# Attention kernel: the row shift as one fp16 row, the closing norm on VectorE in halves, output weights loaded two ahead

## The chip, the cores and the metric

The kernel runs on one core of one Trainium2 chip. The metric is the device time of one execution in microseconds. The kernel before takes 1215.45 us, the median of three runs (1214.27 to 1218.1). One other execution was recorded by the hardware profiler; all views of the profile are of that one.

The engines of the core are called as in the profile: PE (TensorE: matmuls; PEld its weight loads), DVE (VectorE), ACT (ScalarE), POOL (GpSimd) and SP (SyncE, which here only issues DMAs). SP's instructions run in the order of its one queue: an instruction that waits holds up those behind it.

## The reference

One layer of a mixer with two branches: an adaptive layer norm, one input projection, a gated linear recurrence (RG-LRU) on one half of the channels and an attention with a forget gate on the other half, an output projection, a gated residual and a closing layer norm. S = 2048 tokens, D = 1024, eight heads of 64. What the change touches is the attention, the gate on the output weights and the closing norm:

```python
    def block(bi):                      # 128 queries of one block, all heads
        ...
        s = jnp.einsum('bhqd,bhkd->bhqk', qb, k).astype(jnp.float32) * scale
        s = s + (dq[..., :, None] - d_cum[:, :, None, :])
        ...
        s = jnp.where(mask, s, NEG_INF)
        p = jax.nn.softmax(s, axis=-1)
        return jnp.einsum('bhqk,bhkd->bhqd', p.astype(v.dtype), v)
...
        y = jnp.concatenate([y_r, y_a], axis=-1) @ w_out[l]
        res = DEEPNORM_ALPHA * x.astype(jnp.float32) + gate[:, None, :].astype(jnp.float32) * y.astype(jnp.float32)
        x = (_layer_norm(res) * ln_gain[l].astype(jnp.float32) + ln_bias[l].astype(jnp.float32)).astype(dtype)
```

## The kernel before

**Stages.** Up to some 540 us the kernel normalizes x, projects it, runs the recurrence, and writes keys, values, queries and gates to scratch in DRAM (`kd`, `kb`, `vd`, `qd`, `zd`, `yd`). From some 540 us on it runs the attention. Queries are taken in four chunks `ci` of 512 tokens; within a chunk the eight heads `h` come one after the other, 32 items (ci, h) in all. A chunk `ci` sees (ci + 1) x 512 keys.

**One item.** `maxpass` loads the keys of the head: `kk[:, 0]` from `kd` (128 rows of fp16, line 1241) and `kk[0:68, 1]` from `kb` (68 rows, line 1242), then the queries `qb` (line 1243) and `qs` (line 1245). All of these go through SP's queue. The 68 rows of `kb` are 64 rows of the key's head plus four that belong to the row shift and to the forget gate: two rows of the constant RS (written once from `crow`) and two rows `ndr` of the decay, high and low part. The matmuls `pmx` score queries against keys from fp16 parts, VectorE takes each row's maximum (`mc`, line 1259), and lines 1267 to 1269 make the shift of each row: `trow` in fp32, its fp16 high part as column 64 of `Z`, and the rest as column 65. Four transposing matmuls `pzt` bring both columns into rows, and ScalarE copies them into rows 64 and 65 of `qb` (line 1277). These two rows times the RS rows of `kk` then subtract the maximum within the score matmul of `s_t` (`pst<-qb,kk`, 66 rows deep). ScalarE takes the exponential (`pf`, line 1290) and its fp16 part (`ph`, line 1292), GpSimd the low part for three of four tiles (line 1294), VectorE for the fourth (line 1296), and `acc` multiplies by the values.

**Buffers.** Scores, maxima and transposes share five PSUM banks of the tag A. `kk` comes from the pool `r4` (eight buffers of 4 KB per partition) while `ci` is below 2, later from a pool of larger tiles. `r4` also holds the weight tiles `woraw`, the gate `gbc`, the residual tiles `xres` and the gain and bias of the closing norm (`lng`, `lnb`), so that a new tile there waits until the tile that held the buffer is done with.

**Output weights.** `wout_gen` (line 976 on) is a side chain that runs among the first items of the attention. `wo_raw` loads 128 rows of `w_out` (512 KB) and multiplies them by the gate on GpSimd (line 1003); ScalarE and VectorE then split the product into two fp16 parts (lines 880, 881). The next tile is loaded and multiplied before the present one is split: one ahead. `gate_gen` makes the gate itself earlier (adds of line 957).

**Output projection and closing norm.** From some 730 us on, `out_gen` weaves the output projection into the attention, a tile of 128 tokens at a time: `zs` loaded from `zd` (line 1346), multiplied with the transposed attention output on VectorE (line 1369), matmuls `pout`, the residual (line 1468), then `ln_gen`: statistics on VectorE, the reciprocal root on GpSimd (line 1395), `nm` on VectorE (line 1384), the normalization on ScalarE (line 1385, 1024 columns), gain and bias on GpSimd (lines 1387, 1388, 1024 columns each), and the store (line 1389). Fifteen tiles go this way; the last one goes through `out_last`, which does its gain and bias on VectorE.

**What sets the order.** The instructions of each engine stand in the order in which a scheduler places them at build time; the generators above give it the work in the order of their yields, and `issue_after` pins some of it behind a named instruction. VectorE, like every engine, then works in that order: an operation that waits holds up all behind it on its engine.

Of the kernel before, what the change touches and what calls it, by code (L numbers as in the profile page):

```python
# [14 lines left out]
ALU = mybir.AluOpType  # L15
# [23 lines left out]
def hybrid_mixer(  # L39
# [63 lines left out]
            tick()  # L103

    kd = dr.tile([H, P, S], F16, name="kd", tag="kd")
    kb = dr.tile([H, 68, S], F16, name="kb", tag="kb")
    vd = dr.tile([S, C], F32, name="vd", tag="vd")
    qd = dr.tile([H, P, S], F16, name="qd", tag="qd")
    zd = dr.tile([4, P, S], F32, name="zd", tag="zd")
# [755 lines left out]
    nc.vector.tensor_scalar(L8p, sp, 8.0, None, ALU.mult)  # L865
    crow = r4([2, S], "crow", F16)
    nc.vector.memset(crow, RS)
    nc.scalar.dma_start(kb[:, DH:DH + 2, :].rearrange("h a s -> a h s"), crow.unsqueeze(1).broadcast_to([2, H, S]))
    QB = [cst([68, CH], f"qb{i}", F16) for i in range(4)]
    Z = [cst([P, 4, 68], f"Z{i}", F16) for i in range(4)]  # L870
    for q in QB:
        nc.scalar.dma_start(q[66:68, :], crow[:, 0:CH])
    for z in Z:
        nc.gpsimd.memset(z, 0.0)

# [66 lines left out]
    def gate_gen():  # L942
        for k in range(KT):
            raw = r4([P, D], "woraw")
            nc.sync.dma_start(raw, w_out_v[k])
            nc.vector.tensor_reduce(out=wocol[:, k:k + 1], in_=raw, axis=AX.X, op=ALU.max, apply_absolute_value=True)
            if k % 2 == 1:
                yield
        acc = None
        for k in range(KT):  # L950
            w = r4([P, D], "wgate")
            nc.sync.dma_start(w, w_ada_v[k, :, 2 * D:3 * D])
            nc.scalar.activation(w, w, AF.Copy, scale=cact[:, k:k + 1])
            if acc is None:
                acc = w
            else:
                nc.gpsimd.tensor_tensor(out=acc, in0=acc, in1=w, op=ALU.add)
            if k % 2 == 1:
                yield
        gbc = r4([P, D], "gbc")  # L960
        nc.sync.dma_start(gbc, b_ada[0, 2 * D:3 * D].partition_broadcast(P))
        for n in range(2):
            sl = slice(n * CH, (n + 1) * CH)
            ps = bank("C", "pgt")
            mm(ps, ones, acc[:, sl], True, True)
            nc.vector.tensor_tensor(gbc[:, sl], ps, gbc[:, sl], ALU.add)
        gate["bc"] = gbc
        yield
        cols = sm([P, 2], "amg")
        col_max(g_col, AX.X, cols[:, 0:1])  # L970
        col_max(gbc, AX.X, cols[:, 1:2])
        chains.append(gate_fin(cols))
        yield
# [10 lines left out]
    def wout_gen():  # L984
        gbc = gate["bc"]
        wm = sm([P, KT], "wm")
        nc.vector.tensor_tensor(wm, wocol, mk, ALU.mult)
        col = col_max(wm)
        yield
        yield  # L990
        am = yield from all_max(col)
        am_w = sm([P, 1], "am_w")
        nc.vector.tensor_scalar(am_w, am, TINY, gate["am"], ALU.max, ALU.mult)
        scales(am_w, RS, sc_o[:, 1:2], sc_o[:, 0:1])
        nc.vector.tensor_scalar(kap, sc_o[:, 1:2], 1.0 / YT, None, ALU.mult)
        so = cst([P, KT], "so")
        nc.vector.tensor_tensor(so, g_col, mk, ALU.mult)
        nc.vector.tensor_scalar(so, so, sc_o[:, 0:1], 1.0 / ALPHA, ALU.mult, ALU.mult)
        yield
        def wo_raw(k):  # L1000
            raw = r4([P, D], "woraw")
            nc.sync.dma_start(raw, w_out_v[k])
            nc.gpsimd.tensor_tensor(out=raw, in0=raw, in1=gbc, op=ALU.mult)
            return raw

        nxt = wo_raw(0)
        yield
        for k in range(KT):
            raw = nxt
            if k + 1 < KT:  # L1010
                nxt = wo_raw(k + 1)
            w = wh([P, 2, D], "wo") if k < KT - 1 else r4([P, 2, D], "wo", F16)
            for n in range(2):
                sl = slice(n * CH, (n + 1) * CH)
                split_out(w[:, 0, sl], w[:, 1, sl], raw[:, sl], so[:, k:k + 1])
                yield
            wo.append(w)

# [66 lines left out]
    def decay_gen():  # L1085
# [37 lines left out]
        nc.vector.tensor_tensor(ndr[:, 1], ndf, ndr[:, 0], ALU.subtract)  # L1123
        for h in range(H):
            for a in range(2):
                nc.sync.dma_start(kb[h, DH + 2 + a, :].rearrange("(t p) -> t p", p=P), ndr[h * TT:(h + 1) * TT, a, :])
        yield

    dg = decay_gen()
# [101 lines left out]
    def maxpass(ci, h, res):  # L1231
# [10 lines left out]
        nc.sync.dma_start(kk[0:68, 1, 0:nk], kb[h, :, 0:nk])
        nc.sync.dma_start(qb[0:DH, :], qd[h, DH:P, sl])
        qs = sb.tile([P, CH], F16, name="qs", tag="qs", bufs=3)
        nc.sync.dma_start(qs, qd[h, :, sl])
        nc.gpsimd.memset(qb[DH:DH + 2, :], 0.0)
        res.append((kk, qb, qs))
        yield
        mc = sm([P, 4, 4], "mc")
        for i in range(4):  # L1250
            nk = (4 * ci + i + 1) * P
            for b in range(ci + 1):
                w = min(CH, nk - b * CH)
                ps = bank("A", "pmx")
                end = b == ci
                mm(ps[:, 0:w], qb[:, i * P:(i + 1) * P], kk[0:68, 1, b * CH:b * CH + w], True, not end)
                if end:
                    mm(ps[:, w - P:w], identb, maskn, False, True)
                nc.vector.tensor_reduce(out=mc[:, i, b:b + 1], in_=ps[:, 0:w], axis=AX.X, op=ALU.max)  # L1259
                yield  # L1260
# [2 lines left out]
            nc.vector.tensor_reduce(out=m, in_=mc[:, :, 0:ci + 1], axis=AX.X, op=ALU.max)  # L1263
        else:
            m = mc[:, :, 0]
        t = sm([P, 4], "trow")
        nc.vector.tensor_scalar(t, m, -1.0 / RS, ndc[:, ci, h:h + 1], ALU.mult, ALU.add)  # L1267
        nc.vector.tensor_copy(z[:, :, DH], t)  # L1268
        nc.vector.tensor_tensor(z[:, :, DH + 1], t, z[:, :, DH], ALU.subtract)  # L1269
        yield True  # L1270
        yield True
        with tc.issue_after(last["pe"]):
            ps = bank("A", "pzt")
            for i in range(4):
                mm(ps[0:DH + 2, i * P:(i + 1) * P], z[:, i, 0:DH + 2], ident16, i == 0, i == 3, True)
        yield
        nc.scalar.copy(qb[DH:DH + 2, :], ps[DH:DH + 2, :])

    def s_t(ci, h, kt, kk, qb, qs):
        q0 = max(0, kt - 4 * ci) * P  # L1280
# [2 lines left out]
        ps = bank("A", "pst")  # L1283
        mm(ps[:, 0:w], kk[:, 0, ks], qs[:, q0:CH], True, False)
        md = kt >= 4 * ci
        mm(ps[:, 0:w], kk[0:DH + 2, 1, ks], qb[0:DH + 2, q0:CH], False, not md)
        if md:
            mm(ps[:, 0:P], maskn, identb, False, True)
        pf32 = t2([P, CH], "pf32")
# [84 lines left out]
    def ln_gen(tt, xt):  # L1374
        st = sm([P, 2, 6], "bst")
        nc.vector.bn_stats(st[:, 0, :], xt[:, 0:CH])
        yield
        nc.vector.bn_stats(st[:, 1, :], xt[:, CH:D])
        mv = sm([P, 2], "mv")
        nc.vector.bn_aggr(mv, st)  # L1380
        rs = ln_rs(mv)
        yield
        nm = sm([P, 1], "nm")
        nc.vector.scalar_tensor_tensor(nm, mv[:, 0:1], -1.0, rs, ALU.mult, ALU.mult)
        nc.scalar.activation(xt, xt, AF.Identity, scale=rs, bias=nm)  # L1385
        yield
        nc.gpsimd.tensor_tensor(out=xt, in0=xt, in1=late["lng"], op=ALU.mult)
        nc.gpsimd.tensor_tensor(out=xt, in0=xt, in1=late["lnb"], op=ALU.add)
# [230 lines left out]
```

## Time and profile before

| | |
|---|---|
| median of three runs | 1215.45 us (1214.27 to 1218.1) |
| the profiled execution | 1211.64 us |
| its span in the profile | 1209.9 us |
| mean clock granted to TensorE | 0.966 |
| HBM traffic | 97.66 MB read, 31.59 MB written |

A line of the profile that groups instructions reads: line, engine, operation, `out<-in` by the program's names, shape, count | busy us, mean ns of one | idle us of the engine just before them, and what ended most of it. In a list of waits a row reads: engine and line `<-` what it waited for: us in total, times, longest. A row of the timeline reads: start us, us, engine, line, operation, and in square brackets the idle time before it and its releaser. A row of a table by stretches reads: from:to, its length, then busy us of PE, PEld, DVE, ACT and POOL (with instruction counts), the clock granted to TensorE, the mean busy share of the 16 DMA engines, and GB/s. Idle time of an engine that is not the bound costs nothing by itself.

### The profile page before, as it was taken

What the parts mean: (1) busy time and instruction counts of PE and PEld (TensorE: products, weight loads), DVE (VectorE), ACT (ScalarE), POOL (GpSimd) and SP (SyncE); (2) the same over time, 40 slices, a digit from 0 to 9 for tenths busy, and PEclk for the clock granted to TensorE, in tenths of its full rate; (3) what the DMA queues carried; (4) which work ended last, traced back from release to release, by engine and by line L of the source; (5) the groups of instructions that cost most, each with busy time, mean ns of one, the idle gap of its engine ahead of it and who ended that gap; (6) DMA issues with size and microseconds to landing.
All of it is one profiled execution on the core that took longest, in us unless ns stands there. A gap on an engine that the chain in (4) does not pass through costs nothing. (4 is left out here: it accounts for less than half of the span.)

```text
span 1209.9 us, 20217 instructions
## 1 busy us (share of the span) xinstructions
PE 1111.2 (92%) x7467; PEld 622.8 (51%) x7467; DVE 767.7 (63%) x1435; ACT 719.6 (59%) x1244; POOL 686.0 (57%) x670
## 2 busy tenths in 40 slices
PE   6997899999999899999979979989999989999787
PEld 6874444454444444434445545555565555565444
DVE  4378775766668953664396544576677677667534
ACT  3437545564758412623375657577888688888841
POOL 5715532444554300830277645687788689887854
PEclk9998989999999999999979989989999999999899
DMA  9653046221225712754063344222332233221001
GB/s 296 208 151 123 1 118 189 71 64 33 70 70 141 242 55 70 260 160 140 26 205 114 95 129 123 87 93 86 101 94 90 76 103 106 78 89 46 18 27 70
DMA packets 110248, 130.56 MB, mean 108 GB/s; under 512 B 10086, under 2 KB 79318, under 8 KB 110150
## 3 DMA queue, kind: packets, MB, share of 16 engines
q1 hardware_dynamic: 109840, 129.17, 35.0%
q8 instruction: 58, 0.95, 0.3%
q14 instruction: 40, 0.33, 0.1%
q10 hardware_dynamic: 310, 0.12, 0.0%
HBM read 97.66 MB, written 31.59 MB: 107 GB/s over the span
## 5 line engine op out<-in xcount | busy, mean ns | idle before, releaser
L93 PE MATMUL pj<-hT,wT 128*128 128x512 f16 x1440 | 324.4, 383 | 4.1 <-DVE hT L347 1.7
L1294 POOL TENSOR_TENSOR ph<-pf,ph 128x512 f16<-128x512 f32 (+2 forms) x240 | 260.5, 1100 | 67.4 <-ACT ph L1292 62.6
L93 PEld LDWEIGHTS <-wT 128*128 128x128 f16 x1792 | 169.2, 99 | 208.6 <-issue 21.6
L1259 DVE TENSOR_REDUCE mc<-pmx 128x1 f32<-128x512 f32 (+2 forms) x320 | 184.8, 603 | 114.2 <-PE pmx L93 110.0
L1290 ACT ACTIVATE pf<-pst,bias 128x512 f32<-128x512 f32 (+1 forms) x320 | 194.7, 634 | 66.4 <-PE pst L93 58.8
L1292 ACT CAST ph<-pf 128x512 f16<-128x512 f32 (+1 forms) x320 | 171.7, 569 | 20.1 <-PE acc L93 15.9
L93 PE MATMUL acc<-V,ph 128*128 128x129 f16 (+1 forms) x2176 | 158.6, 210 | 22.0 <-POOL ph L1294 14.6
L93 PEld LDWEIGHTS <-ph 128*128 128x128 f16 x2176 | 124.1, 99 | 80.6 <-POOL ph L1294 22.1
L93 PE MATMUL pst<-qs,kk 128*128 128x512 f16 (+1 forms) x320 | 114.3, 360 | 2.0 <-DVE mc L1259 1.3
L93 PE MATMUL pst<-qb,kk 66*128 66x512 f16 (+1 forms) x320 | 112.8, 362 | 0.2
L93 PE MATMUL pmx<-kk,qb 68*128 68x512 f16 (+2 forms) x320 | 105.0, 357 | 7.4 <-DMA kk<-kb 3.8
L93 PE MATMUL pout<-wo,yT 128*128 128x512 f16 (+1 forms) x396 | 95.7, 372 | 1.5 <-ACT yT L1370 1.5
L93 PE MATMUL pout<-wo,yr 128*128 128x512 f16 (+1 forms) x396 | 94.1, 381 | 2.8 <-DVE zs L1369 2.7
L93 PE MATMUL pj<-wN,hT 128*128 128x512 f16 x384 | 89.5, 378 | 0.2 <-ACT XL L814 0.2
L1188 POOL TENSOR_TENSOR XL<-XL,szr 128x512 f32<-128x512 f32 x16 | 24.3, 1522 | 114.7 <-ACT szr L1185 114.7
L1296 DVE TENSOR_TENSOR ph<-pf,ph 128x512 f16<-128x512 f32 (+1 forms) x80 | 64.3, 804 | 33.8 <-ACT ph L1292 33.2
L93 PEld LDWEIGHTS <-kk 66*128 66x128 f16 (+1 forms) x640 | 55.1, 100 | 34.5 <-issue 11.6
L93 PE MATMUL pq<-hT,wT 128*128 128x512 f16 x288 | 67.0, 379 | 2.8 <-DVE qhl L881 2.8
L93 PEld LDWEIGHTS <-hT 128*128 128x128 f16 x640 | 44.5, 97 | 48.3 <-issue 3.6
L93 PEld LDWEIGHTS <-yr 128*128 128x128 f16 x396 | 38.3, 100 | 42.8 <-issue 8.0
L93 PEld LDWEIGHTS <-yT 128*128 128x128 f16 x396 | 37.5, 98 | 39.4 <-ACT yT L1370 1.7
L483 POOL TENSOR_TENSOR xl<-xc,xh 128x512 fp32r<-128x512 f32 x16 | 24.4, 1532 | 57.8 <-ACT xh L481 47.0
(307 smaller groups left out, 1846.0 us busy)
## 6 DMA issues: line engine op xcount, KB each, us to landing
wraw<-in_w_in_dram SPq DMA_DIRECT2D x40, 512.0 KB
woraw<-in_w_out_dram SPq DMA_DIRECT2D x16, 512.0 KB
xres<-in_x_dram SPq DMA_DIRECT2D x16, 512.0 KB
out_dram<-xres SPq DMA_DIRECT2D x15, 512.0 KB
wadab<-in_w_ada_dram SPq DMA_DIRECT2D x8, 512.0 KB
xt<-in_x_dram SPq DMA_DIRECT2D x16, 256.0 KB
xt<-in_x_dram SPq DMA_DIRECT2D x8, 512.0 KB
wsh<-in_w_ada_dram SPq DMA_DIRECT2D x16, 256.0 KB
```

The source lines that it names most:

```text
L93: m = nc.tensor.matmul(o, lhsT=l, rhs=r, start=st, stop=sp, skip_group_check=chk)
L483: nc.gpsimd.tensor_tensor(out=xl, in0=xc, in1=xh, op=ALU.subtract)
L1188: nc.gpsimd.tensor_tensor(out=XL[j][:, sl], in0=XL[j][:, sl], in1=sz, op=ALU.mult)
L1259: nc.vector.tensor_reduce(out=mc[:, i, b:b + 1], in_=ps[:, 0:w], axis=AX.X, op=ALU.max)
L1290: nc.scalar.activation(pf32[:, 0:w], ps[:, 0:w], AF.Exp, scale=DH ** -0.5, bias=bias[:, ci, h, kt:kt + 1])
L1292: nc.scalar.copy(ph[:, 0, 0:w], pf32[:, 0:w])
L1294: nc.gpsimd.tensor_tensor(out=ph[:, 1, 0:w], in0=pf32[:, 0:w], in1=ph[:, 0, 0:w], op=ALU.subtract)
L1296: nc.vector.tensor_tensor(ph[:, 1, 0:w], pf32[:, 0:w], ph[:, 0, 0:w], ALU.subtract)
```

## The change

Three parts. (1) The row shift becomes one fp16 row: line 1267 writes column 64 of `Z` directly, the cast and the subtraction go, `pzt` and the copy handle one row, and one row of RS goes from `kb`, which then has 67 rows in DRAM, in the loads and in the `pmx` matmuls. (2) In `ln_gen` the normalization with gain and bias is done by four VectorE operations on 512 columns: (x − mean) · gain twice, then · rs + bias twice. ScalarE's and GpSimd's three passes go. (3) `wout_gen` loads the weights two ahead and multiplies by the gate in halves, between the two halves of the split; the adds of `gate_gen` are done in halves too.

```diff
@@ -103,7 +103,7 @@
             tick()
 
     kd = dr.tile([H, P, S], F16, name="kd", tag="kd")
-    kb = dr.tile([H, 68, S], F16, name="kb", tag="kb")
+    kb = dr.tile([H, 67, S], F16, name="kb", tag="kb")
     vd = dr.tile([S, C], F32, name="vd", tag="vd")
     qd = dr.tile([H, P, S], F16, name="qd", tag="qd")
     zd = dr.tile([4, P, S], F32, name="zd", tag="zd")
@@ -865,11 +865,11 @@
     nc.vector.tensor_scalar(L8p, sp, 8.0, None, ALU.mult)
     crow = r4([2, S], "crow", F16)
     nc.vector.memset(crow, RS)
-    nc.scalar.dma_start(kb[:, DH:DH + 2, :].rearrange("h a s -> a h s"), crow.unsqueeze(1).broadcast_to([2, H, S]))
-    QB = [cst([68, CH], f"qb{i}", F16) for i in range(4)]
+    nc.scalar.dma_start(kb[:, DH:DH + 1, :].rearrange("h a s -> a h s"), crow[0:1].unsqueeze(1).broadcast_to([1, H, S]))
+    QB = [cst([67, CH], f"qb{i}", F16) for i in range(4)]
     Z = [cst([P, 4, 68], f"Z{i}", F16) for i in range(4)]
     for q in QB:
-        nc.scalar.dma_start(q[66:68, :], crow[:, 0:CH])
+        nc.scalar.dma_start(q[65:67, :], crow[:, 0:CH])
     for z in Z:
         nc.gpsimd.memset(z, 0.0)
 
@@ -954,7 +954,9 @@
             if acc is None:
                 acc = w
             else:
-                nc.gpsimd.tensor_tensor(out=acc, in0=acc, in1=w, op=ALU.add)
+                for n in range(2):
+                    sl = slice(n * CH, (n + 1) * CH)
+                    nc.gpsimd.tensor_tensor(out=acc[:, sl], in0=acc[:, sl], in1=w[:, sl], op=ALU.add)
             if k % 2 == 1:
                 yield
         gbc = r4([P, D], "gbc")
@@ -1000,19 +1002,26 @@
         def wo_raw(k):
             raw = r4([P, D], "woraw")
             nc.sync.dma_start(raw, w_out_v[k])
-            nc.gpsimd.tensor_tensor(out=raw, in0=raw, in1=gbc, op=ALU.mult)
             return raw
 
-        nxt = wo_raw(0)
-        yield
+        def wo_gate(raw):
+            for n in range(2):
+                sl = slice(n * CH, (n + 1) * CH)
+                nc.gpsimd.tensor_tensor(out=raw[:, sl], in0=raw[:, sl], in1=gbc[:, sl], op=ALU.mult)
+
+        raws = [wo_raw(0), wo_raw(1)]
+        yield
+        wo_gate(raws[0])
         for k in range(KT):
-            raw = nxt
-            if k + 1 < KT:
-                nxt = wo_raw(k + 1)
+            raw = raws.pop(0)
             w = wh([P, 2, D], "wo") if k < KT - 1 else r4([P, 2, D], "wo", F16)
             for n in range(2):
                 sl = slice(n * CH, (n + 1) * CH)
                 split_out(w[:, 0, sl], w[:, 1, sl], raw[:, sl], so[:, k:k + 1])
+                if n == 0 and k + 2 < KT:
+                    raws.append(wo_raw(k + 2))
+                if n == 0 and k + 1 < KT:
+                    wo_gate(raws[0])
                 yield
             wo.append(w)
 
@@ -1123,7 +1132,7 @@
         nc.vector.tensor_tensor(ndr[:, 1], ndf, ndr[:, 0], ALU.subtract)
         for h in range(H):
             for a in range(2):
-                nc.sync.dma_start(kb[h, DH + 2 + a, :].rearrange("(t p) -> t p", p=P), ndr[h * TT:(h + 1) * TT, a, :])
+                nc.sync.dma_start(kb[h, DH + 1 + a, :].rearrange("(t p) -> t p", p=P), ndr[h * TT:(h + 1) * TT, a, :])
         yield
 
     dg = decay_gen()
@@ -1239,11 +1248,11 @@
         else:
             kk = sb.tile([P, 2, S], F16, name="kk", tag="H", bufs=8)
         nc.sync.dma_start(kk[:, 0, 0:nk], kd[h, :, 0:nk])
-        nc.sync.dma_start(kk[0:68, 1, 0:nk], kb[h, :, 0:nk])
+        nc.sync.dma_start(kk[0:67, 1, 0:nk], kb[h, :, 0:nk])
         nc.sync.dma_start(qb[0:DH, :], qd[h, DH:P, sl])
         qs = sb.tile([P, CH], F16, name="qs", tag="qs", bufs=3)
         nc.sync.dma_start(qs, qd[h, :, sl])
-        nc.gpsimd.memset(qb[DH:DH + 2, :], 0.0)
+        nc.gpsimd.memset(qb[DH:DH + 1, :], 0.0)
         res.append((kk, qb, qs))
         yield
         mc = sm([P, 4, 4], "mc")
@@ -1253,7 +1262,7 @@
                 w = min(CH, nk - b * CH)
                 ps = bank("A", "pmx")
                 end = b == ci
-                mm(ps[:, 0:w], qb[:, i * P:(i + 1) * P], kk[0:68, 1, b * CH:b * CH + w], True, not end)
+                mm(ps[:, 0:w], qb[:, i * P:(i + 1) * P], kk[0:67, 1, b * CH:b * CH + w], True, not end)
                 if end:
                     mm(ps[:, w - P:w], identb, maskn, False, True)
                 nc.vector.tensor_reduce(out=mc[:, i, b:b + 1], in_=ps[:, 0:w], axis=AX.X, op=ALU.max)
@@ -1263,18 +1272,15 @@
             nc.vector.tensor_reduce(out=m, in_=mc[:, :, 0:ci + 1], axis=AX.X, op=ALU.max)
         else:
             m = mc[:, :, 0]
-        t = sm([P, 4], "trow")
-        nc.vector.tensor_scalar(t, m, -1.0 / RS, ndc[:, ci, h:h + 1], ALU.mult, ALU.add)
-        nc.vector.tensor_copy(z[:, :, DH], t)
-        nc.vector.tensor_tensor(z[:, :, DH + 1], t, z[:, :, DH], ALU.subtract)
+        nc.vector.tensor_scalar(z[:, :, DH], m, -1.0 / RS, ndc[:, ci, h:h + 1], ALU.mult, ALU.add)
         yield True
         yield True
         with tc.issue_after(last["pe"]):
             ps = bank("A", "pzt")
             for i in range(4):
-                mm(ps[0:DH + 2, i * P:(i + 1) * P], z[:, i, 0:DH + 2], ident16, i == 0, i == 3, True)
-        yield
-        nc.scalar.copy(qb[DH:DH + 2, :], ps[DH:DH + 2, :])
+                mm(ps[0:DH + 1, i * P:(i + 1) * P], z[:, i, 0:DH + 1], ident16, i == 0, i == 3, True)
+        yield
+        nc.scalar.copy(qb[DH:DH + 1, :], ps[DH:DH + 1, :])
 
     def s_t(ci, h, kt, kk, qb, qs):
         q0 = max(0, kt - 4 * ci) * P
@@ -1283,7 +1289,7 @@
         ps = bank("A", "pst")
         mm(ps[:, 0:w], kk[:, 0, ks], qs[:, q0:CH], True, False)
         md = kt >= 4 * ci
-        mm(ps[:, 0:w], kk[0:DH + 2, 1, ks], qb[0:DH + 2, q0:CH], False, not md)
+        mm(ps[:, 0:w], kk[0:DH + 1, 1, ks], qb[0:DH + 1, q0:CH], False, not md)
         if md:
             mm(ps[:, 0:P], maskn, identb, False, True)
         pf32 = t2([P, CH], "pf32")
@@ -1380,12 +1386,15 @@
         nc.vector.bn_aggr(mv, st)
         rs = ln_rs(mv)
         yield
-        nm = sm([P, 1], "nm")
-        nc.vector.scalar_tensor_tensor(nm, mv[:, 0:1], -1.0, rs, ALU.mult, ALU.mult)
-        nc.scalar.activation(xt, xt, AF.Identity, scale=rs, bias=nm)
-        yield
-        nc.gpsimd.tensor_tensor(out=xt, in0=xt, in1=late["lng"], op=ALU.mult)
-        nc.gpsimd.tensor_tensor(out=xt, in0=xt, in1=late["lnb"], op=ALU.add)
+        for n in range(2):
+            ns = slice(n * CH, (n + 1) * CH)
+            nc.vector.scalar_tensor_tensor(xt[:, ns], xt[:, ns], mv[:, 0:1], late["lng"][:, ns], ALU.subtract, ALU.mult)
+            yield
+        for n in range(2):
+            ns = slice(n * CH, (n + 1) * CH)
+            nc.vector.scalar_tensor_tensor(xt[:, ns], xt[:, ns], rs, late["lnb"][:, ns], ALU.mult, ALU.add)
+            if n == 0:
+                yield
         nc.sync.dma_start(out[tt * P:(tt + 1) * P, :], xt)
 
     def ln_rs(mv):
```

The order in which the engines get the work, at three places. First SP's queue late in the attention, where three loads of keys for the last chunk stand ahead of a `zs`; names are tiles with their numbers. Before:

```order
397 L1241 DMA kk_11385<-kd_63 128x2048
398 L1242 DMA kk_11385<-kb_64 68x2048
399 L1241 DMA kk_11790<-kd_63 128x2048
400 L1242 DMA kk_11790<-kb_64 68x2048
401 L1241 DMA kk_12186<-kd_63 128x2048
402 L1242 DMA kk_12186<-kb_64 68x2048
403 L1346 DMA zs_11263<-zd_67 128x4x128
```

The same place after:

```order
400 L1250 DMA kk_11308<-kd_63 128x2048
401 L1251 DMA kk_11308<-kb_64 67x2048
402 L1250 DMA kk_11711<-kd_63 128x2048
403 L1251 DMA kk_11711<-kb_64 67x2048
404 L1250 DMA kk_12105<-kd_63 128x2048
405 L1251 DMA kk_12105<-kb_64 67x2048
406 L1355 DMA xres_12681<-in_x_dram 128x1024
407 L1352 DMA zs_11193<-zd_67 128x4x128
```

The three pairs and the `zs` keep their places, with 67 rows for 68; a load of a residual tile now stands ahead of `zs`.

Second, SP's queue early in the attention, at the last loads of output weights, with the semaphores that each row waits for (`Pool_...` is GpSimd, `DMAHW...` an earlier DMA of the same semaphore). Before, from the last weight tile on:

```order
348 L1002 DMA woraw_6555<-in_w_out_dram 128x1024 [waits DMAHW2_49,PE_49]
349 L1243 DMA qb1_1605<-qd_66 64x512 [waits DMAHW3_49]
350 L887 DMA qd_66<-qhl_6681 64x512 [waits DMAHW4_49,Activation_49]
351 L887 DMA qd_66<-qhl_6681 64x512 [waits DMAHW5_49]
352 L889 DMA qd_66<-qhl_6681 64x512 [waits DMAHW6_49,DVE_49]
353 L889 DMA qd_66<-qhl_6681 64x512 [waits DMAHW7_49]
354 L1241 DMA kk_6780<-kd_63 128x1024 [waits DMAHW0_49,Pool_49]
355 L1242 DMA kk_6780<-kb_64 68x1024 [waits DMAHW1_49]
```

After, from the last weight tile on:

```order
332 L1004 DMA woraw_6384<-in_w_out_dram 128x1024 [waits DMAHW2_49,PE_49]
333 L1252 DMA qb0_1604<-qd_66 64x512 [waits DMAHW3_49]
334 L1250 DMA kk_6490<-kd_63 128x1024 [waits DMAHW4_49,Pool_49]
335 L1251 DMA kk_6490<-kb_64 67x1024 [waits DMAHW5_49]
336 L1250 DMA kk_7780<-kd_63 128x1536 [waits DMAHW6_49]
337 L1251 DMA kk_7780<-kb_64 67x1536 [waits DMAHW7_49]
338 L1250 DMA kk_8062<-kd_63 128x1536 [waits DMAHW0_49,PE_49]
```

The last weight load stands earlier in the queue, and the load of keys that waits for GpSimd is that of item (1, 3) (`kk_6490`) where it was that of item (1, 4) (`kk_6780`); keys for the third chunk (`kk_7780`, `kk_8062`) are queued behind it.

Third, VectorE's queue in the last chunk, around the closing norm of one tile. Before:

```order
1161 L1314 RECIPROCAL rv_11087<-ytmp_11085 128x2
1162 L1259 TENSOR_REDUCE mc_11002<-pmx_11097 128x1
1163 L1314 RECIPROCAL rv_11093<-ytmp_11091 128x2
1164 L1384 SCALAR_TENSOR_TENSOR nm_11267<-mv_11033,rs_11037 128x1
1165 L1259 TENSOR_REDUCE mc_11002<-pmx_11118 128x1
1166 L1259 TENSOR_REDUCE mc_11002<-pmx_11121 128x1
```

After, at a like tile:

```order
1200 L1272 TENSOR_REDUCE mrow_12007<-mc_11718 128x4
1201 L1386 BN_AGGR mv_12064<-bst_11819 128x2
1202 L1275 TENSOR_SCALAR Z0_1608<-mrow_12007,ndc_3534 128x4
1203 L1402 TENSOR_SCALAR ve_12066<-mv_12064 128x1
1204 L1391 SCALAR_TENSOR_TENSOR xres_11195<-xres_11195,mv_12064,lng_7042 128x512 x2
1205 L1395 SCALAR_TENSOR_TENSOR xres_11195<-xres_11195,rs_12068,lnb_7044 128x512 x2
1206 L1268 TENSOR_REDUCE mc_12112<-pmx_12113 128x1
```

Where one operation on one column (`nm`) stood between reductions, four of 512 columns now stand ahead of the next reduction; the shift of the rows is one operation (line 1275).

## The prediction

> **What bounds the kernel now.** I read the busy shares first, then stretches of 100 us over the attention stage, then the waits of that stage.
>
> ```profile
> PE 1111.2 (92%) x7467; PEld 622.8 (51%) x7467; DVE 767.7 (63%) x1435; ACT 719.6 (59%) x1244; POOL 686.0 (57%) x670
> ```
>
> ```profile
> core 0: us, PE busy (x) PEld busy (x) DVE busy (x) ACT busy (x) POOL busy (x), PEclk, DMA share, GB/s
> 1000.00:1100.00 100.00, 99.19 (x885) 58.62 (x884) 70.44 (x128) 82.19 (x154) 85.97 (x82) 1.00 0.25 84
> ```
>
> TensorE is the bound: 92% busy over the span and 99% in 1000 to 1100. Whatever makes it wait adds to the time, and there is little idle time left to win. The next view is the list of waits between 585 and 1205 us (total, times, longest):
>
> ```profile
> DVE mc L1259 <- PE pmx L93: 110.0, 92, 7.6
> PE acc L93 <- POOL ph L1294: 14.6, 20, 3.5
> POOL woraw L1003 <- DMA woraw<-in_w_out_dram: 14.3, 5, 7.6
> PE pzt L93 <- DVE Z L1269: 9.1, 10, 2.3
> PE pmx L93 <- DMA kk<-kb: 3.8, 3, 1.5
> ```
>
> VectorE waits 110 us for TensorE, so it has room on average. TensorE's own waits that the change aims at are the 9.1 us for Z and part of the 14.6 us for ph. The kb loads already end late three times.
>
> **Row shift.** Three small VectorE operations per head (lines 1267 to 1269) become one; the two that go:
>
> ```profile
> L1268 DVE CAST Z<-trow 128x4 f16<-128x4 f32 x32 | 14.5, 454 | 0.5
> L1269 DVE TENSOR_TENSOR Z<-trow,Z 128x4 f16<-128x4 f32 x32 | 18.4, 574 | 0.9
> ```
>
> That is 14.5 + 18.4 = 33 us of VectorE, and two of the three steps between the last reduction and pzt. On the path that is two thirds of the 9.1 us: **−6 us**. The memset and the copy of one row instead of two work on 512 columns as before and give nothing.
>
> **Closing norm.** ScalarE's pass and GpSimd's two go, and VectorE gets four operations of 512 columns for each of 15 tiles:
>
> ```profile
> L1385 ACT ACTIVATE xres<-xres,nm,rs 128x1024 f32<-128x1024 f32 x15 | 18.8, 1251 | 16.8 <-DVE nm L1384 16.7
> L1387 POOL TENSOR_TENSOR xres<-xres,lng 128x1024 f32<-128x1024 f32 x15 | 35.4, 2357 | 9.6 <-ACT xres L1385 9.2 <-PE pmx L93 0.4
> L1388 POOL TENSOR_TENSOR xres<-xres,lnb 128x1024 f32<-128x1024 f32 x15 | 35.3, 2352 | 0.3
> L1468 DVE SCALAR_TENSOR_TENSOR xres<-pout,kap,xres 128x512 f32<-128x512 f32 x30 | 22.4, 747 | 28.1 <-PE pout L93 27.9
> ```
>
> By line 1468's 0.747 us the 60 new operations cost 44.8 us of VectorE; with nm and lines 1268 and 1269 gone its sum rises by some 8 us, well inside its 110 us of waiting. GpSimd loses 70.7 us, ScalarE 18.8. What TensorE sees is the delay of ph behind a 2.36 us block. Bounds: −14.6 (all its waits for GpSimd's ph) and +23, if each tile holds the reductions back by two operations (15 x 2 x 0.75). I take **−4**, near the lower cost, since only every fifth or so of those waits stands beside lines 1387 and 1388.
>
> What the two engines do to each other shows here (timeline):
>
> ```profile
> 936.96 2.36 POOL L1388 TENSOR_TENSOR xres<-xres,lnb 128x1024 f32<-128x1024 f32 x1
> 937.08 2.27 DVE L1269 TENSOR_TENSOR Z<-trow,Z 128x4 f16<-128x4 f32 x1
> 939.41 0.64 PE L93 MATMUL pzt<-ident,Z 128*66 128x128 f16 x4 [1.64 <-DVE Z L1269]
> ```
>
> A VectorE operation on 4 columns lasts until GpSimd's is done, and TensorE pays 1.64 us. The Trainium skill ("SBUF — State Buffer", section "SBUF: two separate sides") says why: the pair of ports that the two share is an exclusive lock, taken also by a VectorE operation with two SBUF inputs against a GpSimd one that reads SBUF. The row agrees. By that rule the closing operations, whose two tensors both lie in SBUF, only move the collisions; the sum would be 4 us higher.
>
> **Output weights.** In 696 to 711 GpSimd waits for a weight load, ph stands behind it, and TensorE waits:
>
> ```profile
> 704.27 2.34 POOL L1003 TENSOR_TENSOR woraw<-woraw,gbc 128x1024 f32<-128x1024 f32 x1 [7.65 <-DMA woraw<-in_w_out_dram]
> 707.29 0.56 PE L93 MATMUL acc<-V,ph 128*128 128x65 f16 x5 [3.53 <-POOL ph L1294]
> 710.94 0.58 PE L93 MATMUL pmx<-kk,qb 68*128 68x512 f16 x1 [1.21 <-DMA kk<-kb]
> ```
>
> Loading two ahead should take away the 3.53 and some of what follows, 5 us. But now the kk of the item before (order of SyncE) waits for GpSimd's last gate product, with a weight load in front: I give 2 back, so **−3**; bounds −7 and +3. Behind that waiting load SyncE's queue holds kb of the same head, kk of two later heads and yr; if the gates come late, all of them do. The gate adds of line 957 are the same work in halves, ahead of the attention stage, and no wait of TensorE in the list names them: nothing. So far the three parts give −13.
>
> **The 67 rows.** The fp16 row makes kb 67 rows where it was 68, and all 32 kk<-kb loads change shape. How many DMA engines share such a load is seen where it is the only traffic:
>
> ```profile
> 707.60:708.60 1.00, 0.25 (x4) 0.03 (x1) 1.00 (x2) 1.00 (x3) 1.00 (x1) 0.50 0.90 225
> 836.00:837.00 1.00, 1.00 (x16) 0.76 (x15) 1.00 (x3) 1.00 (x3) 1.00 (x1) 1.00 0.27 108
> 1001.00:1004.00 3.00, 3.00 (x20) 1.41 (x19) 3.00 (x3) 3.00 (x7) 3.00 (x2) 1.00 0.25 102
> ```
>
> While the 128-row load of 707.6 runs, 0.90 of the 16 engines work. While only 68-row loads are left (the two lower rows), it is 0.25 to 0.27: four engines, 102 GB/s, about 25.5 each. 128 rows divide by 16, and 68 by 4 but by nothing greater up to 16; so the number of engines looks like the greatest divisor of the rows up to 16. 67 is prime: one engine. The Trainium skill ("DMA: Bandwidth & Descriptors", section "Why a DMA increments its semaphore by 16 and not by 1") states this rule and names 127 partitions as a case of one engine; the 0.25 for 68 rows agrees, and no run here yet shows a prime.
>
> The greatest and the smallest of four sizes before (2048, 1536, 1024 and 512 columns, eight loads each):
>
> ```profile
> kk<-kb SPq DMA_DIRECT2D x8, 272.0 KB
> kk<-kb SPq DMA_DIRECT2D x8, 68.0 KB
> ```
>
> With 67 of 68 rows that is 69, 137, 206 and 274 kB: at 25.5 GB/s 2.7, 5.4, 8.1 and 10.8 us instead of a quarter of it, so 2.0, 4.0, 6.1 and 8.1 us more each. That engine's share of every load behind it comes later too, and a load is done when its slowest share is. Most kk loads are issued a head or more early, and this is hidden. Where it is not:
>
> Three kb loads, then zs:
>
> ```profile
> 991.43 0.33 SPq L1242 DMA_DIRECT2D kk<-kb  x1
> 993.00 0.38 SPq L1242 DMA_DIRECT2D kk<-kb  x1
> 1004.18 0.38 SPq L1346 DMA_DIRECT2D zs<-zd  x1
> 1012.97 0.68 DVE L1369 TENSOR_TENSOR zs<-pyt,zs 128x512 f32<-128x512 f32 x1
> ```
>
> The third stands between the two, at 992.18. They kept four engines busy until 1004 (share 0.25 above); 3 x 8.1 = 24 us more is 1028, and VectorE takes zs at 1012.97: 15 us late. VectorE works in order, so the reductions of pmx stand behind line 1369 and TensorE runs out of banks; five banks of 0.38 us matmuls let it go on for some 2 us. **+13.**
>
> Two kb loads, then zs:
>
> ```profile
> 829.22 0.32 SPq L1242 DMA_DIRECT2D kk<-kb  x1
> 829.96 0.32 SPq L1242 DMA_DIRECT2D kk<-kb  x1
> 830.38 0.94 SPq L1346 DMA_DIRECT2D zs<-zd  x1
> 838.00:839.00 1.00, 0.38 (x5) 0.13 (x2) 0.96 (x4) 1.00 (x3) 1.00 (x2) 1.00 0.16 47
> 841.75 0.68 DVE L1369 TENSOR_TENSOR zs<-pyt,zs 128x512 f32<-128x512 f32 x1
> ```
>
> Done at some 838.7 now (0.16 of that microsecond), 12.2 later is 851, against 841.75: 9 late, **+7**. One kb load, of 204 KB, right ahead of zs:
>
> ```profile
> 869.12 0.38 SPq L1346 DMA_DIRECT2D zs<-zd  x1
> 874.00:875.00 1.00, 0.79 (x3) 0.29 (x3) 1.00 (x3) 1.00 (x3) 1.00 (x1) 1.00 0.16 52
> 876.64 0.68 DVE L1369 TENSOR_TENSOR zs<-pyt,zs 128x512 f32<-128x512 f32 x1
> ```
>
> 875 + 6.1 = 881, 4 late: **+2**.
>
> ```profile
> 730.02 0.38 SPq L1346 DMA_DIRECT2D zs<-zd  x1
> 737.24 0.67 DVE L1369 TENSOR_TENSOR zs<-pyt,zs 128x512 f32<-128x512 f32 x1
> 777.16 0.43 PE L93 MATMUL pmx<-kk,qb 68*128 68x512 f16 x2 [1.52 <-DMA kk<-kb]
> ```
>
> The first zs stands right behind a 204 KB kb load and is used 7.2 us after its issue; 6.1 later, less the cover of 2: **+4**. At 777.16 TensorE already waits for kb, so the 4.0 is paid whole: **+4**. The wait at 710.94 grows by its own 4.0 and by the two 204 KB loads ahead of it: 4 to 12, and the third wait for kb, of the head before, has 4 more; together **+12**. For the first heads, where qb stands behind the kb load, at most 8 x 2.0: I take **+4**. Sum: 13 + 7 + 2 + 4 + 4 + 12 + 4 = 46.
>
> **The sum.** −13 + 46 = +33 on the profiled execution's 1211.6 us: 1244.6. The median shown lies 3.8 us above that execution; I carry it over: **1248 us**.
>
> **Rivals.**
> - *The transfers cost nothing*, because 67 rows are spread after all, or because every load is early enough. For it: in 1000 to 1100 the engines are busy only 0.25 of the time. Against it: the four-engine rows, and zs taken at 1012.97, nine microseconds after its issue, with three loads ahead. It decides if the share during a kb load does not fall to 0.06. Then 1211.6 − 13 + 3.8 = **1202**, faster. Chance 0.13.
> - *Only the three waits that exist today grow* (3 x 4.0 = 12), since zs is issued earlier than now: 1211.6 − 13 + 12 + 3.8 = **1214**, no change. Chance 0.07.
> - *VectorE's blocks of closing operations hold up the reductions*, at the +23 above instead of −4, with the late transfers beside it: 1248 + 27 = **1275**. For it: ScalarE and GpSimd are busier than VectorE, and each new operation may wait for GpSimd. Against it: 110 us of VectorE's waiting. Chance 0.1.
> - *The late engine adds up*: beyond the seven places kk and qb come late too. All extra transfer time is 8 x (2.0 + 4.0 + 6.1 + 8.1) = 162 us; a third of it paid instead of 46 is 54 or more, and each stall pushes later loads together: **1260 to 1290**. Chance 0.15.
> - The forecast keeps 0.55.
>
> **Range and chances.** 1210 to 1290 leaves out most of the first rival and little above. A measurement of this kernel tells 0.3%, 3.6 us, from no change. Faster 0.13, same 0.07, slower 0.80.
>
> **What will show it.** The DMA share during the tail of a kb load falls to 0.06 at about 25 GB/s; TensorE's and VectorE's waits name kk<-kb, zs and qb with many microseconds (zs near 850 and 1030 above all); the wait of pzt for Z falls to about a third; GpSimd's sum falls by 70 us; the weight wait near 700 is gone or now stands at kk. Wrong would be a share that stays at 0.25 or rises, or TensorE's new waits on mc rather than on transfers.

## The result and the profile after

The changed kernel takes 1282.88 us (median of 4 runs, 1279.07 to 1283.54) beside 1214.86 before: ratio 1.0549, interval 1.0505 to 1.0593. That is 68 us more, where 33 were forecast; the time lies in the range, 35 us above the forecast.

The busy shares of the profiled execution (1283.39 us, span 1281.7):

```profile
PE 1117.5 (87%) x7467; PEld 624.7 (49%) x7467; DVE 772.6 (60%) x1416; ACT 706.4 (55%) x1229; POOL 627.3 (49%) x655
```

GpSimd has lost 59 us (70 forecast) and ScalarE 13, and still TensorE fell from 92% to 87%. The list of waits from 585 us on says for what (total, times, longest):

```profile
DVE zs L1375 <- DMA zs<-zd: 48.9, 4, 19.3
PE pout L93 <- DVE zs L1375: 43.0, 5, 19.0
PE pmx L93 <- DMA kk<-kb: 22.8, 4, 8.4
PE pmx L93 <- DMA kk<-kd: 11.2, 1, 11.2
PE acc L93 <- POOL ph L1300: 10.3, 22, 1.6
PE pzt L93 <- DVE Z L1275: 2.9, 2, 1.9
```

Before, the rows for zs (2.7 at TensorE) and kk (3.8) were small. Now TensorE loses 43.0 + 22.8 + 11.2 = 77 us to transfers. The wait for Z fell from 9.1 to 2.9, that for GpSimd's ph from 14.6 to 10.3. These gains came; the transfers cost several times as much.

The table by stretches shows a stretch of 3 us in which one kb load of 2048 columns is all the traffic there is, and one of 4 us with a load of 1024 columns, in which every engine waits:

```profile
943.00:946.00 3.00, 3.00 (x27) 1.68 (x26) 3.00 (x5) 2.41 (x4) 3.00 (x5) 1.00 0.06 26
800.00:804.00 4.00, 0.00 (x0) 0.00 (x0) 0.00 (x0) 0.00 (x0) 0.00 (x0) 0.57 0.07 26
```

The last two columns are the point: 0.06 is one of 16 engines, and it moves 26 GB/s, where the 68 rows had 0.25 and 102. The greatest-divisor rule of the prediction and its rate of 25.5 GB/s were right. These rows also agree with the rule of the Trainium skill ("DMA: Bandwidth & Descriptors", section "Why a DMA increments its semaphore by 16 and not by 1"), which gives four engines for 68 rows and one for the prime 67.

SyncE's timeline and the two waits at the place with three kb loads ahead of a zs:

```profile
1045.11 0.72 SPq L1251 DMA_DIRECT2D kk<-kb  x1
1046.56 0.31 SPq L1251 DMA_DIRECT2D kk<-kb  x1
1046.91 10.74 SPq L1250 DMA_DIRECT2D kk<-kd  x1
1057.70 0.28 SPq L1251 DMA_DIRECT2D kk<-kb  x1
1058.08 12.06 SPq L1355 DMA_DIRECT2D xres<-in_x_dram  x1
1070.19 1.04 SPq L1352 DMA_DIRECT2D zs<-zd  x1
1086.50 0.69 DVE L1375 TENSOR_TENSOR zs<-pyt,zs 128x512 f32<-128x512 f32 x1 [19.33 <-DMA zs<-zd]
1087.24 1.01 PE L93 MATMUL pout<-wo,yr 128*128 128x512 f16 x2 [19.04 <-DVE zs L1375]
```

Two things are to be seen. Issues of a DMA that took a third of a microsecond before take 10.74 and 12.06: SyncE itself stands still while the kb loads run on the one engine, and meanwhile the DMA share falls to 0.07 (1052 to 1057) and 0.06 (1064 to 1070). And of the 19.33 us that VectorE waits, TensorE pays 19.04: there is almost no cover.

TensorE's timeline, the matmuls that had to wait for a transfer (in brackets, with what ended the wait); the stalls shift the later places against the times of before:

```profile
618.04 0.27 PE L93 MATMUL pmx<-kk,qb 67*128 67x128 f16 x1 [2.33 <-DMA kk<-kb]
...
638.90 0.27 PE L93 MATMUL pmx<-kk,qb 67*128 67x128 f16 x1 [4.90 <-issue]
...
701.43 0.58 PE L93 MATMUL pmx<-kk,qb 67*128 67x512 f16 x1 [11.15 <-DMA kk<-kd]
...
730.57 0.59 PE L93 MATMUL pmx<-kk,qb 67*128 67x512 f16 x1 [7.87 <-DMA kk<-kb]
...
764.00 5.28 PE L93 MATMUL pout<-wo,yr 128*128 128x512 f16 x12 [6.76 <-DVE zs L1375]
...
804.56 0.69 PE L93 MATMUL pmx<-kk,qb 67*128 67x512 f16 x2 [8.38 <-DMA kk<-kb]
...
876.41 0.58 PE L93 MATMUL pmx<-kk,qb 67*128 67x512 f16 x1 [4.19 <-DMA kk<-kb]
...
888.56 4.00 PE L93 MATMUL pout<-wo,yr 128*128 128x512 f16 x9 [10.91 <-DVE zs L1375]
...
927.53 4.09 PE L93 MATMUL pout<-wo,yr 128*128 128x512 f16 x12 [5.87 <-DVE zs L1375]
```

With the 19.04 above these are all the places of the forecast and one more (876.41). The wait at 638.90 is put down to no releaser; it stands among the first heads, and I count it there.

### The profile page after: what moved, and what is told of

Same layout as the page of the kernel before. It is cut to its first block, busy times and chain, and to the rows that moved or that the text cites. A ratio compares the mean times of both kernels' runs of the same rounds, so it can differ in the third digit from the quotient of the medians.

```text
span 1281.7 us, 20209 instructions
## 1 busy us (share of the span) xinstructions
PE 1117.5 (87%) x7467; PEld 624.7 (49%) x7467; DVE 772.6 (60%) x1416; ACT 706.4 (55%) x1229; POOL 627.3 (49%) x655
## 5 line engine op out<-in xcount | busy, mean ns | idle before, releaser
L1300 POOL TENSOR_TENSOR ph<-pf,ph 128x512 f16<-128x512 f32 (+2 forms) x240 | 266.2, 1122 | 112.8 <-ACT ph L1298 100.3
L1298 ACT CAST ph<-pf 128x512 f16<-128x512 f32 (+1 forms) x320 | 172.4, 567 | 12.8 <-PE acc L93 6.7
L93 PE MATMUL acc<-V,ph 128*128 128x129 f16 (+1 forms) x2176 | 159.5, 210 | 17.3 <-POOL ph L1300 10.3
L93 PE MATMUL pmx<-kk,qb 67*128 67x512 f16 (+2 forms) x320 | 106.3, 366 | 43.3 <-DMA kk<-kb 22.8
L93 PE MATMUL pout<-wo,yr 128*128 128x512 f16 (+1 forms) x396 | 99.5, 399 | 43.0 <-DVE zs L1375 43.0
L93 PE MATMUL pst<-qb,kk 65*128 65x512 f16 (+1 forms) x320 | 112.7, 361 | 0.1
L1302 DVE TENSOR_TENSOR ph<-pf,ph 128x512 f16<-128x512 f32 (+1 forms) x80 | 56.8, 709 | 40.4 <-ACT ph L1298 34.3
L93 PEld LDWEIGHTS <-kk 65*128 65x128 f16 (+1 forms) x640 | 54.9, 100 | 50.6 <-issue 28.2
L93 PE MATMUL pj<-h,w 128*128 128x512 f32 x192 | 50.1, 411 | 2.0 <-ACT h L380 2.0
```

The costliest lines, as they stand in the source:

```text
L93: m = nc.tensor.matmul(o, lhsT=l, rhs=r, start=st, stop=sp, skip_group_check=chk)
L1298: nc.scalar.copy(ph[:, 0, 0:w], pf32[:, 0:w])
L1300: nc.gpsimd.tensor_tensor(out=ph[:, 1, 0:w], in0=pf32[:, 0:w], in1=ph[:, 0, 0:w], op=ALU.subtract)
L1302: nc.vector.tensor_tensor(ph[:, 1, 0:w], pf32[:, 0:w], ph[:, 0, 0:w], ALU.subtract)
```

## The experiments

All compute the whole of the reference. Ratios are to the kernel before, measured in the same series on the same chip. The median of that kernel lay between 1214.86 and 1218.76 us in the five series, so a difference of a few microseconds between kernels of two series is uncertain, and the ratios tell more than the times.

| kernel | median us | ratio | interval |
|---|---|---|---|
| a_split: the change, kb loads in 64 + 3 rows | 1201.86 | 0.9867 | 0.9845 to 0.9889 |
| b_67_1: before, kb loads in 67 + 1 rows | 1291.98 | 1.0612 | 1.0579 to 1.0645 |
| a_split_late: the change, split in chunks 2 and 3 | 1226.37 | 1.0066 | 1.0043 to 1.0089 |
| a_split_early: the change, split in chunks 0 and 1 | 1261.56 | 1.0362 | 1.0333 to 1.0391 |
| b_split: before, kb loads in 64 + 4 rows | 1213.51 | 0.9973 | 0.9946 to 1.0 |
| p_row: row shift alone, 64 + 3 | 1192.95 | 0.9795 | 0.9755 to 0.9835 |
| p_cl: closing norm alone, 64 + 4 | 1211.54 | 0.9947 | 0.9918 to 0.9975 |
| p_wo: output weights alone, 64 + 4 | 1225.84 | 1.0073 | 1.0046 to 1.01 |
| p_rowcl: row shift and closing norm, 64 + 3 | 1193.74 | 0.982 | 0.9789 to 0.9851 |
| p_wohalf: the weights' halves alone, 64 + 4 | 1212.79 | 1.0001 | 0.9968 to 1.0034 |
| a_zs_act: the change, zs from ScalarE's queue | 1252.2 | 1.0298 | 1.0261 to 1.0334 |
| a_68: the change, kb padded to 68 rows | 1210.98 | 0.9959 | 0.9936 to 0.9981 |
| p_row3: p_row with the two VectorE operations back | 1214.33 | 0.9973 | 0.9938 to 1.0008 |

### Is it the 67 rows?

a_split takes the prime number out of the changed kernel:

```diff
-        nc.sync.dma_start(kk[0:67, 1, 0:nk], kb[h, :, 0:nk])
+        nc.sync.dma_start(kk[0:64, 1, 0:nk], kb[h, 0:64, 0:nk])
+        nc.sync.dma_start(kk[64:67, 1, 0:nk], kb[h, 64:67, 0:nk])
```

> The changed kernel with each kk<-kb load in two: 64 rows and 3 rows, so that no load is 67 rows on one DMA engine; nothing else differs. Theory (the loss is the late 67-row loads and what stands behind them): the 75 us of TensorE's new waits for kk and zs go, the time is 1195 to 1212, and the three parts show their own worth beside 1215. Rival (the loss is in VectorE's closing operations or in the order of the weights): above 1245.

b_67_1 brings it into the kernel before, with nothing else of the change:

```diff
-        nc.sync.dma_start(kk[0:68, 1, 0:nk], kb[h, :, 0:nk])
+        nc.sync.dma_start(kk[0:67, 1, 0:nk], kb[h, 0:67, 0:nk])
+        nc.sync.dma_start(kk[67:68, 1, 0:nk], kb[h, 67:68, 0:nk])
```

> The kernel before with each kk<-kb load of 68 rows in two: 67 rows and 1 row; nothing of the change. Theory: the same one DMA engine carries it all, so the loss of some 75 us comes without any of the change's three parts: 1275 to 1300. Rival (the parts cost it): 1215 to 1230.

1201.9 and 1292.0: both as the theory had it. The list of waits of a_split has hardly anything left for zs, and 9.2 for kk (5.8 of it at one place, where the output weights come in; see below):

```profile
PE pmx L93 <- DMA kk<-kb: 9.2, 3, 5.8
PE pout L93 <- DVE zs L1376: 1.9, 4, 0.9
```

and TensorE is back at 92% of the span:

```profile
PE 1107.9 (92%) x7467; PEld 622.8 (52%) x7467; DVE 777.6 (65%) x1416; ACT 705.3 (59%) x1229; POOL 629.7 (52%) x655
```

The list of b_67_1 has the late zs and kk again, without the changes. It also has a late place of its own: GpSimd waits for transfers ahead of its gate products, and TensorE then waits for GpSimd's ph, 27.9 us where it was 14.6 before:

```profile
PE pout L93 <- DVE zs L1370: 36.5, 6, 16.4
POOL woraw L1003 <- DMA qd<-qhl: 23.5, 2, 16.7
PE acc L93 <- POOL ph L1295: 27.9, 18, 12.6
PE pmx L93 <- DMA kk<-kb: 16.5, 3, 6.0
```

So the loss is the transfer's row count: 81.0 us between the changed kernel and a_split, and 73 for b_67_1 above the before of its series (1218.76). Without it the change is a gain of 1.3%.

### Where is it paid?

a_split_late and a_split_early split the loads of only two chunks each (`if ci >= 2:`, `if ci < 2:`).

> The changed kernel, loads of the chunks 2 and 3 (1536 and 2048 columns) in 64 + 3 rows, those of the chunks 0 and 1 left at 67. Theory: the zs waits (43 us) and one kk wait (4) go, some 20 to 35 us of kk waits before 805 us stay: 1222 to 1240. Rival (the first stage costs nothing, only zs does): 1200 to 1212.

> The converse: loads of the chunks 0 and 1 in 64 + 3 rows, those of the chunks 2 and 3 at 67. Theory: the zs waits stay, with the part of the kk waits before 735 us that two loads of chunk 2 cause: 1245 to 1268; the excess of this kernel and of a_split_late over a_split adds up to that of the changed kernel within 15. Rival: the early lateness is what moves the later loads together, and the zs waits shrink with it: below 1235.

1226.4 and 1261.6, inside both expectations: 24.5 us for the early chunks and 59.7 for the late ones over a_split; 84 together, against 81.0. The waits divide likewise; 9.2 us of each kk row stand in a_split too. Of a_split_late:

```profile
PE pmx L93 <- DMA kk<-kb: 26.6, 4, 11.4
```

and of a_split_early:

```profile
PE pout L93 <- DVE zs L1379: 43.5, 6, 19.0
PE pmx L93 <- DMA kk<-kb: 19.0, 5, 6.0
```

Early, TensorE waits for the keys themselves; late, for zs behind them in the queue. It was 26 for the late places in the forecast (13 + 7 + 2 + 4) and 20 for the early ones.

### Does zs wait for its place in the queue, or for the engine?

a_zs_act leaves all 67-row loads and issues zs from ScalarE's queue (`nc.scalar.dma_start` in `prep_a`).

> The changed kernel with its 67-row loads, zs loaded from ScalarE's DMA queue instead of SyncE's. Open: whether zs waits for its place in SyncE's queue, behind issues of up to 12 us and kb's descriptors, or for the one DMA engine. Theory (the place in the queue): zs waits fall from 49 to below 15, and the time to 1235 to 1255. Rival (the engine is shared whatever the queue): waits and time stay, above 1268.

```profile
PE pmx L93 <- DMA kk<-kb: 28.9, 4, 10.9
DVE zs L1375 <- DMA zs<-zd: 21.8, 7, 4.8
PE pout L93 <- DVE zs L1375: 17.5, 7, 5.0
```

The time, 1252.2, lies where the theory put it, 31 us below the changed kernel; the waits for zs fell from 48.9 to 21.8, not below 15. The longest is 4.8 where it was 19.3. At the place with the 19.3, zs was issued 25.1 us after the first of the kb loads ahead of it (1045.11 to 1070.19) and taken 16.3 us after its issue. In a_zs_act it was issued 14.3 us after that load (1030.29 to 1044.56) and taken 10.0 us later. So most of what was won there is the earlier issue: mainly, zs waited for its place in SyncE's queue. What is left goes with the engine that its loads still share with kb; no run tests that part alone. The Trainium skill ("DMA: Bandwidth & Descriptors", section "Queues, rings and completion order") has each engine take its queues in turn, packet by packet; the shorter but not vanished waits agree.

a_68 pads kb to 68 rows and loads it whole.

> The changed kernel with kb padded by one row to 68 (a copy of the RS row that no matmul reads), loaded whole as before the change: four DMA engines again. Theory: the prime number is all that matters, so 1200 to 1210, within 8 us of a_split at 1201.9. Rival (what costs is that the loads are not on all 16 engines): 1215 or more.

It came out at 1211.0, one microsecond above the theory's bound and below the rival's. Its wait list:

```profile
PE pmx L93 <- DMA kk<-kb: 12.2, 4, 7.3
PE pout L93 <- DVE zs L1376: 6.1, 3, 5.0
```

The row count explains most (72 of 81 us), but four engines cost the changed kernel 9 us against 64 + 3 rows (11 by the ratios): 3.0 at kk and 4.2 at zs in these rows.

### What are the three parts worth?

b_split is the base of the parts: the kernel before with loads of 64 + 4 rows. Each part stands on it (or on 64 + 3).

> The kernel before with each kk<-kb load of 68 rows in 64 + 4 rows: nothing of the change, but the loads use all DMA engines. Theory: only the waits of the profile before go (kk 3.8, zs 2.7), so 0 to 7 us faster than before, 0.994 to 1.0. Rival (four engines already cost more than these waits): 0.99 or lower.

> The row shift alone, kb loads in 64 + 3 rows. Theory: 6 us below b_split, for two thirds of the 9.1 us wait of pzt for Z. Rival: no difference from b_split within 2 us, since the wait moves to the next operation.

> The closing norm on VectorE alone, kb loads of 68 rows in 64 + 4. Theory: 4 us below b_split. Rivals: none (the exclusive pair of ports only moves the collisions), within 2 us of b_split; or the blocks hold up the reductions, 5 to 23 us above b_split.

> The output weights loaded two ahead alone, kb loads of 68 rows in 64 + 4. Theory: 3 us below b_split. Rival: the wait of the keys for GpSimd's gates replaces the one removed, 0 to 3 us above b_split.

b_split is 0.27% faster by ratio, its interval touching 1.0: within the theory. Against its 1213.5 the row shift gives −20.6 us (−6 expected), the closing norm −2.0 (−4), the weights +12.3 (−3). Added, −10.3; a_split lies 11.7 below b_split, so the parts add up within what two series can tell.

**Closing norm.** The intervals of p_cl and b_split overlap, so neither a gain nor its absence is shown. In p_cl the new operations take:

```profile
L1390 DVE SCALAR_TENSOR_TENSOR xres<-xres,rs,lnb 128x512 f32<-128x512 f32 x30 | 31.4, 1074 | 1.8 <-POOL rs L1399 1.8
L1386 DVE SCALAR_TENSOR_TENSOR xres<-xres,mv,lng 128x512 f32<-128x512 f32 x30 | 26.9, 935 | 0.0
L1472 DVE SCALAR_TENSOR_TENSOR xres<-pout,kap,xres 128x512 f32<-128x512 f32 x30 | 22.4, 748 | 21.2 <-PE pout L93 20.2 <-PE acc L93 0.9
```

The two with both tensors in SBUF need 1.07 and 0.94 us, the one that reads PSUM 0.75 for the same size. It is not the operation itself that is slower: the same one in `out_last`, at the kernel's end, where the timeline shows no GpSimd operation beside it, takes 0.75 as well:

```profile
L1433 DVE SCALAR_TENSOR_TENSOR xres<-xres,rs,lnb 128x512 f32<-128x512 f32 x2 | 1.4, 747 | 0.0
```

This agrees with the exclusive lock of the Trainium skill ("SBUF — State Buffer", section "SBUF: two separate sides"). The measured −2.0 lies halfway between the −4 of the forecast and the nothing that the prediction took from that rule, so it does not decide between them.

**Output weights.** The timeline of p_wo at its worst place, GpSimd, SyncE, TensorE:

```profile
694.58 2.48 POOL L1010 TENSOR_TENSOR woraw<-woraw,gbc 128x512 f32<-128x512 f32 x2 [0.59 <-DMA woraw<-in_w_out_dram]
697.09 0.33 SPq L1250 DMA_DIRECT2D kk<-kd  x1
697.46 0.46 SPq L1251 DMA_DIRECT2D kk<-kb  x1
700.62 0.59 PE L93 MATMUL pmx<-kk,qb 68*128 68x512 f16 x1 [6.02 <-DMA kk<-kb]
```

The gate product ends at 697.06, the load of keys that stands next in SyncE's queue is issued at 697.09, and TensorE waits 6.02 us for it. It is the new wait that the prediction priced at 2. Is it the load two ahead or the halves? p_wohalf has the halves alone (the gate adds of line 957 are halved as in the change):

```diff
-            nc.gpsimd.tensor_tensor(out=raw, in0=raw, in1=gbc, op=ALU.mult)
+            for n in range(2):
+                sl = slice(n * CH, (n + 1) * CH)
+                nc.gpsimd.tensor_tensor(out=raw[:, sl], in0=raw[:, sl], in1=gbc[:, sl], op=ALU.mult)
```

> Of the weights' part the halves alone (gate product and gate adds in 512 columns), still loaded one ahead, kb loads in 64 + 4 rows. p_wo was 12 us above b_split. Theory (the load two ahead costs it, by the wait of the keys for the gate product, 6.0 us in p_wo): within 4 us of b_split, 1209 to 1217. Rival (twice as many operations on GpSimd cost it): 1220 or more.

1212.8: the halves cost nothing that can be measured, the load two ahead costs the 12 (9 by the ratios of the two series). Six of them stand in the row above. The other six were not traced to one wait; TensorE is busy 1115.8 us in p_wo and 1109.7 in b_split for the same number of matmuls, at a granted clock of 0.961 and 0.966.

**Row shift.** Why 20.6 and not 6? p_row3 is p_row with the removed cast and subtraction put back (into a column that the scores do not use) and pzt waiting for all three.

> Open: the row shift alone is worth 20.6 us (p_row against b_split) where 6 were forecast for the shorter chain on VectorE. This kernel is p_row with the two removed VectorE operations put back (cast and subtraction into a column of Z that the scores don't use, pzt waits for all three), everything else at one row; VectorE's order is that of b_split. Theory (all of it comes from the shorter VectorE chain, with what a waiting TensorE triggers): 1208 to 1216, as b_split. Rival (the chain is worth the 6 forecast, the rest is the order of loads and matmuls that changed with it): 1195 to 1202 if the order stays as in p_row, or 1208 and more with the wait of pzt for Z at 9 us or less if the order of b_split comes back; the profile's stretch 600 to 700 tells: TensorE 82 busy in b_split, 91 in p_row.

1214.3, as b_split: the whole gain goes when the two operations come back, so it hangs on the VectorE chain, not on the single row in loads and scores (the transposes carry both columns again). The waits of pzt are 3.8 us in p_row and 11.0 in p_row3, which is 7 of the 20. Most of the rest is in TensorE's own matmuls, busy 1103.3 us in p_row and 1114.8 in p_row3 for the same number of them. The stretch 600 to 700 shows a part of it, first p_row:

```profile
600.00:700.00 100.00, 91.10 (x729) 53.67 (x728) 63.49 (x139) 71.93 (x154) 73.47 (x90) 0.95 0.51 149
```

then p_row3:

```profile
600.00:700.00 100.00, 81.47 (x594) 46.67 (x593) 64.62 (x142) 59.88 (x131) 64.63 (x81) 0.86 0.39 118
```

TensorE does 729 matmuls there instead of 594, and the granted clock is 0.95 instead of 0.86. Putting the operations back also brings back the order of b_split on VectorE, so how much of the 13 us beyond pzt's wait is that order and how much the lower clock was not separated.

### The best version

> Row shift and closing norm, without the output weights' part, kb loads in 64 + 3 rows: what the runs so far point to as the best version. Theory (the parts add: row 21 us and closing 2 us below b_split at 1213.5): 1188 to 1194, 0.975 to 0.981 of before. Rival (each part's gain hangs on the order of the others, as the weights' loss did): 1196 or more.

p_rowcl has 1193.7 us and 0.982: the time inside the theory's bounds, the ratio just outside. The closing norm gives nothing that can be measured on top of the row shift. **p_row, the row shift with kb loads in 64 + 3 rows, has the lowest median of the kernels run**, 2% below before; its interval and that of p_rowcl overlap, so the two are not told apart.

## Why the prediction was right and wrong

- **What bounds the kernel**: right. Of the 48.9 us that VectorE waited for zs, TensorE paid 43.0.
- **The 67 rows**: the mechanism, its rate and its places were right; the size was not. This is the step that failed: "13 + 7 + 2 + 4 + 4 + 12 + 4 = 46" measured 81.0 (the changed kernel against a_split). Place by place, the waits in the changed kernel's timeline, those of a_split at the same place taken off where there are any:

| place | forecast | measured |
|---|---|---|
| zs behind three kb loads | 13 | 19.0 |
| zs behind two, with kk just ahead of it | 7 | 10.9 + 4.2 − 0.4 = 14.7 |
| zs behind one | 2 | 5.9 |
| first zs | 4 | 6.8 − 0.2 = 6.6 |
| kk that waited 1.52 | 4 | 8.4 − 2.8 = 5.6 |
| the other two waits for kb | 12 | 11.2 − 5.8 + 7.9 = 13.3 |
| first heads | 4 | 2.3 − 0.7 + 4.9 = 6.5 |

  They sum to some 71. The other 10 us go with TensorE's own work, busy 1117.5 us against 1107.9 in a_split for the same number of matmuls, at a granted clock of 0.94 against 0.966; the forecast had no term for that. Of the 25 us by which the waits were missed, 20 stand at the four zs places, and three assumptions failed there. The cover of "some 2 us" at each late zs was hardly there: TensorE paid 19.04 of 19.33 us, and 10.91 behind the 4.19 for kk just before it at the second. The loads were priced as if issued as early as before, but SyncE was held for up to 12 us by its own issues: from the first of the three kb loads to the zs behind them it took 12.8 us before (991.43 to 1004.18) and 25.1 now. And kk waits that were hidden before (4.2 ahead of the second zs) came up, as the fourth rival had it.

  The three rows for keys came out nearer. At the first of the "other two waits", 5.8 of the 11.2 us are not the 67 rows' at all: a_split waits as long there (at 691.05), as p_wo does (6.02, above), and no kernel with 64 + 3 or 64 + 4 rows that leaves out the weights' load two ahead has a kk wait above 2.8. It is the wait that the output weights bring, which the prediction had in that part's term:

```profile
691.05 0.58 PE L93 MATMUL pmx<-kk,qb 67*128 67x512 f16 x1 [5.83 <-DMA kk<-kb]
```

  At the 1.52 us wait TensorE came 2.3 us after the issue of kb before, and 0.1 us after it now (issue at 796.08, TensorE idle from 796.18 to 804.56). It did so in a_split too (766.46 and 766.60), so this comes with the three parts, not with the 67 rows.
- **The three parts**: "−13" measured −11.7 (a_split against b_split), right only by luck, because the errors cancel: −20.6 for "−6", −2.0 for "−4", +12.3 for "−3". The row shift's term counted only the wait that the list names; the weights' term named the right new wait and priced a third of the one row that shows it.
- **The rivals**: "transfers cost nothing, 1202" is what a_split measures, 1201.9, but only with the row count mended, and with the −13 that is right by luck. That VectorE's blocks hold up the reductions at +23 is not seen: p_cl is no slower than b_split. "The late engine adds up, 1260 to 1290" came nearest, by its time and by its reason.

## What to carry to other kernels

Look at the row count of a DMA before the bytes: loads that got 1.5% smaller went from four engines to one and cost 81 us, 6.7% of the time of a_split, and splitting them into 64 + 3 rows turned the same change into a gain. When a transfer gets longer, price it by what stands behind it in its queue and by where the waiting engine stands, not by its own extra time; once the queue's issues are held, the lateness no longer has the distances of the old trace. And test the parts of a change apart: here one gave 20 us, one nothing that could be measured, and one took 12.

## What the runs showed of the hardware that was not expected

- Behind two loads of 67 rows the next issue on SyncE took 10.74 us, and behind a third one 12.06, where those in front of the same zs took 0.32 to 0.58 before. Nothing else was issued on SyncE's queue meanwhile, though the DMA share was down to 0.07 and 0.06 for part of that time. What ends such an issue was not tested.
- The same late zs load from ScalarE's queue was issued earlier and landed sooner: the longest wait was 4.8 us, not 19.3.
- A VectorE operation with both tensors in SBUF (p_cl, 512 columns) takes 0.94 to 1.07 us on average among GpSimd's work and 0.75 without it, which is also the time of one that reads PSUM.
- Putting two small operations back into VectorE's chain (and with them the old order) went with a clock granted to TensorE of 0.86 instead of 0.95 over 600 to 700 us.
